# Predicting an edit: three projections opened during the modulation of a hybrid SSD and convolution layer

## The chip, the cores and the metric

One Trainium2 chip, one of its cores. The metric is the device time of one execution in microseconds (us); lower is better. Engines are named as the profile does: PE is TensorE, DVE VectorE, ACT ScalarE, POOL GpSimd, SP SyncE.

## What is computed

One trunk layer over 512 latent tokens and 256 context tokens of 1024 channels, fp32. The edit concerns its first steps:

```
mod   = silu(c) @ w_mod + b_mod          # the same for the context with c_ctx; split in shift, scale, gate
h     = rms_norm(x, norm_w) * (1 + scale) + shift
h_ctx = the same for the context tokens
proj  = h @ w_in                         # dt (step sizes), xs, B, C, z, glu, cg, gates; h_ctx @ w_in for dt, xs, B
dt    = softplus(dt_raw + dt_bias);  la = cumsum(dt * a) within chunks of 128
```

Behind them come a bidirectional state space mixer in eight groups of heads, a convolution module, gates, an output projection, the residual and a last norm. All that is the same in both kernels.

## The kernel before, in words

Everything is one function, `hybrid_block`. A scheduler puts the instructions of each engine into one fixed order when the program is built, and each engine then runs its own list in order.

*The start.* The modulation weights come in four blocks (`load_mod`, L198) of 1024 x 512: 256 channels of shift and of scale. SP loads block 0, the tokens `xt`, block 1, the context `ct`, block 2, and later block 3 and the first weights. For each block q, PE multiplies the two conditioning vectors (padded to 4 columns, `scf`) with the weights into `mp` (L249), DVE copies it to `ms` (L251), four transposes (`tp`, L254) bring it to the partitions, and DVE adds halves and bias (`md`) and makes the scale `s` (L263). Meanwhile ACT squares the tokens (L223), `rsqrt_small` makes the root, ACT scales the tokens (L227, L229). Then, for each of the two 128-channel blocks k of q, PE transposes the tokens (`hp`, L267), ACT (tokens, L272) or DVE (context, L270) applies scale and shift into `hf`, and `split` (L163, L164) makes a rounded fp32r half on ACT and its remainder on DVE: `hx[0]`, `hx[1]`, `hc[0]`, `hc[1]`.

*The projections.* `proj` (L322) takes a weight block of 128 output channels (`wblock`, L149: a rounded half `whi` on ACT, the remainder `wlo` on DVE) and sums over all eight k: three 512-column products for the tokens (L330, L331, L335) and, where the context is needed, three of 256 columns (L333, L334, L337). Two accumulators `px` and one `pc` are in rotation. The order of weight blocks is dt, then for each group xs, xs, B, C, z, z and so on.

*The step sizes.* From dt's sums ACT and DVE go through some ten small steps (L348 to L365), PE transposes and sums them (`tpd`, `pl`, `lt`, `pr`, `pt`, L370 to L394), `la` goes through DRAM, and ACT makes `wend` and `dec` (L398 to L402). Then the first group's `conv` copies xs0's and xs1's accumulators out (`pad`, L160).

Of the kernel before, what the change touches and what calls it, by code (L numbers as in the profile page):

```python
# [46 lines left out]
SPLIT_K = ()  # L47
# [32 lines left out]
def hybrid_block(ctx: ExitStack, tc: tile.TileContext, x, cx, pack, wmod, bgate, wall, fnw, out):  # L80
# [15 lines left out]
    def pv(name):  # L96
        o, w = OFF[name]
        return pk[:, o:o + w]
# [94 lines left out]
    with tc.tile_pool(name="st", bufs=1, reuse_waits="tile") as st, tc.tile_pool(name="stp", bufs=1, space=PSUM) as stp:  # L193
        xt = st.tile([P, NCH, D], F32, name="xt")
        ct = st.tile([P, NCC, D], F32, name="ct")
        wms = []

        def load_mod(q):  # L198
            wm = st.tile([P, KO, 512], F32, name="wm", tag="wm", bufs=3)
            for hf in range(2):  # L200
                nc.sync.dma_start(out=wm[:, 4 * hf:4 * hf + 4], in_=wmod[q, :, hf * 2048:(hf + 1) * 2048].rearrange("p (k c) -> p k c", k=4))
            wms.append(wm)

        load_mod(0)
        for t in range(0, NCH, 2):
            nc.sync.dma_start(out=xt[:, t:t + 2], in_=x[t * P:(t + 2) * P, :].rearrange("(t p) d -> p t d", p=P))
        load_mod(1)
        nc.sync.dma_start(out=ct, in_=cx.rearrange("(t p) d -> p t d", p=P))
        load_mod(2)
        sc = st.tile([P, KO, 2], F32, name="sc")  # L210
        table = S.activation(sc, pv("cT").rearrange("p (k two) -> p k two", two=2), AF.Silu)
        S.copy(scs[:, :, 0], sc)
        V.tensor_sub(scs[:, :, 1], sc, scs[:, :, 0].bitcast(F32))
        scf = st.tile([P, KO, 2, 2], F32, name="scf")
        V.memset(scf, 0.0)
        V.tensor_copy(scf[:, :, 0], sc)
        table = log_exp_table(table)
        ss = st.tile([P, NCH + NCC], F32, name="ss")
        junk = st.tile([P, D], F32, name="junk", tag="junk", bufs=2)
        for t in range(NCH + NCC):  # L220
            src = xt[:, t] if t < NCH else ct[:, t - NCH]
            junk = st.tile([P, D], F32, name="junk", tag="junk", bufs=2)
            S.activation(junk, src, AF.Square, accum_out=ss[:, t:t + 1])  # L223
        rx = rsqrt_small(st, "rx", ss[:, 0:NCH], 1.0 / D, table)
        rc = rsqrt_small(st, "rc", ss[:, NCH:], 1.0 / D, table)
        for t in range(NCH):
            S.mul(xt[:, t], xt[:, t], rx[:, t:t + 1])  # L227
        for t in range(NCC):
            S.mul(ct[:, t], ct[:, t], rc[:, t:t + 1])  # L229

        for q in range(4):
            if q == 1:
                load_mod(3)
                prefetch()
                prefetch()
            wm = wms[q]
            mp = stp.tile([4, 512], F32, name="mp", tag="mp", bufs=2)
            for k in range(0, KO, 2):
                if k in SPLIT_K:
                    wmh = st.tile([P, 2, 512], F32R, name="wmh", tag="wmh", bufs=2)  # L240
                    wml = st.tile([P, 2, 512], F32R, name="wml", tag="wml", bufs=2)
                    split(wmh, wml, wm[:, k:k + 2])
                for j in range(2):
                    if k in SPLIT_K:
                        st_ = scs[:, k + j].rearrange("p a b -> p (a b)")
                        T.matmul(mp, st_, wmh[:, j], start=(k + j == 0), stop=False)
                        T.matmul(mp, st_, wml[:, j], start=False, stop=(k + j == KO - 1))
                    else:
                        T.matmul(mp, scf[:, k + j].rearrange("p a b -> p (a b)"), wm[:, k + j], start=(k + j == 0), stop=(k + j == KO - 1))  # L249
            ms = st.tile([4, 512], F32, name="ms", tag="ms", bufs=2)  # L250
            V.tensor_copy(ms, mp)  # L251
            tp = stp.tile([P, 2, 2, 2, 2], F32, name="tp", tag="tp", bufs=1)
            for j in range(4):
                T.transpose(tp[:, j // 2, j % 2].rearrange("p a b -> p (a b)"), ms[:, j * P:(j + 1) * P], ident[0:4, 0:4])  # L254
            td = st.tile([P, 2, 2, 2, 2], F32, name="td", tag="td", bufs=2)
            V.tensor_copy(td, tp)
            md = st.tile([P, 2, 2, 2], F32, name="md", tag="md", bufs=2)
            V.tensor_add(md, td[:, :, :, 0], td[:, :, :, 1])
            V.tensor_add(md, md, pv("bmod").rearrange("p (s k) -> p s k", s=2)[:, :, 2 * q:2 * q + 2].unsqueeze(3).broadcast_to([P, 2, 2, 2]))
            for j in range(2):  # L260
                k = 2 * q + j
                s1 = st.tile([P, 2], F32, name="s1", tag="s1", bufs=4)
                V.tensor_scalar(s1, md[:, 1, j, :], 1.0, pv("normw")[:, k:k + 1], op0=ALU.add, op1=ALU.mult)  # L263
                for which, srct, n, dst in ((0, xt, NCH, hx), (1, ct, NCC, hc)):
                    hp = stp.tile([P, n * P], F32, name=f"hp{which}", tag=f"hp{which}", bufs=2)
                    for t in range(n):
                        T.transpose(hp[:, t * P:(t + 1) * P], srct[:, t, k * P:(k + 1) * P], ident)  # L267
                    hf = st.tile([P, n * P], F32, name=f"hf{which}", tag=f"hf{which}", bufs=2)
                    if which:
                        V.tensor_scalar(hf, hp, s1[:, which:which + 1], md[:, 0, j, which:which + 1], op0=ALU.mult, op1=ALU.add)  # L270
                    else:
                        S.activation(hf, hp, AF.Identity, scale=s1[:, which:which + 1], bias=md[:, 0, j, which:which + 1])  # L272
                    split(dst[0][:, k, :], dst[1][:, k, :], hf)

# [8 lines left out]
    taps = []  # L283
# [38 lines left out]
    def proj(pool, kind, idx, with_ctx=False, psx=None):  # L322
# [5 lines left out]
        for k in range(KO):  # L328
# [7 lines left out]
            if with_ctx:  # L336
                T.matmul(pc, lo[:, k, :], hc[0][:, k, :], start=False, stop=last)  # L337
        return px, pc

    if True:  # L340
        pp_stack = ctx
        pp = pp_stack.enter_context(tc.tile_pool(name="pp", bufs=1, space=PSUM, reuse_waits="tile"))
# [507 lines left out]
```

## Time and profile before

| what | us |
|---|---|
| runs, median of 3 (lowest, highest) | 947.39 (946.71, 948.42) |
| the profiled execution, span from first to last instruction | 945.1 |
| PE busy within the span | 923.5 |
| first modulation product | 6.52 |
| first projection product (dt) | 47.86 |
| first product of B | 73.78 |

The profile gives the profiled execution's time as its span; the runs' median is 2.3 us above it, which is what lies around the span. An engine's busy time is the time in which at least one of its instructions is in flight. Matmuls overlap each other, so a product's own length is longer than its step, the time from its start to the next one's.

### The profile page before, as it was taken

The page shows a single profiled execution, that of the slowest core. Times are in us where ns is not written, and L with a number is a line of the kernel's source. Part 1 is how long each engine was busy: PE and PEld are TensorE (multiplying, and loading weights), DVE is VectorE, ACT ScalarE, POOL GpSimd, SP SyncE. Part 2 cuts the span into 40 slices and gives each one's busy share as a digit, 9 for nine tenths or more (in the row PEclk, how much of TensorE's full clock was granted, in tenths as well). Part 3 has the DMA queues.
Part 4 walks back from the last instruction along what each step waited for, and adds up shares of the span by engine and source line. Part 5 has one row for each costly group of instructions (what it writes and reads, how often), then busy time and mean ns, then how long its engine had stood idle before and what let it go on. Part 6 is the DMA issues. An engine that isn't in the chain of part 4 may idle for free.

```text
span 945.1 us, 12712 instructions
## 1 busy us (share of the span) xinstructions
PE 923.5 (98%) x4695; PEld 735.2 (78%) x4695; DVE 735.6 (78%) x1232; ACT 529.5 (56%) x935; POOL 9.2 (1%) x115
## 2 busy tenths in 40 slices
PE   6999999999999999999999999999999999999996
PEld 1388788788788788787887887788888877778886
DVE  1667499997699994899994999789999964557933
ACT  5738946767667668468477667444523345424322
POOL 0000000000000000000000000000000000000000
PEclk9999999999999999999999999999999999999999
DMA  9524512512422324225124122366633345647622
GB/s 375 204 77 139 178 46 88 169 68 93 142 68 99 116 96 152 75 68 179 44 91 178 34 84 95 127 200 209 201 113 132 114 163 179 200 153 268 203 77 80
DMA packets 41376, 127.07 MB, mean 134 GB/s; under 512 B 4545, under 2 KB 4961, under 8 KB 40290
## 3 DMA queue, kind: packets, MB, share of 16 engines
q1 hardware_dynamic: 25040, 93.22, 28.5%
q10 hardware_dynamic: 16274, 33.04, 10.1%
q8 instruction: 37, 0.61, 0.3%
q14 instruction: 25, 0.20, 0.1%
HBM read 112.46 MB, written 13.78 MB: 134 GB/s over the span
## 4 chain that ended last, share of the span: by engine, by line
PE 84%; ACT 11%; DMA 3%; issue 2%; DVE 1%; SPq 0%; ACTq 0%
PE px L331 14%; PE px L335 14%; PE px L330 14%; PE px L764 5%; PE yo L568 3%; PE po L608 3%; PE po L607 3%; PE po L606 3%; PE mp L249 3%; ACT el L490 3%; PE pc L333 2%; PE pc L337 2%; PE pc L334 2%; PE yd L561 2%; ACT whi L154 2%; PE cp L529 2%
## 5 line engine op out<-in xcount | busy, mean ns | idle before, releaser
L330 PE MATMUL px<-hx,whi 128*128 128x512 f32 x712 | 284.9, 400 | 0.0
L331 PE MATMUL px<-hx,whi 128*128 128x512 f32 x712 | 282.4, 397 | 0.0
L335 PE MATMUL px<-hx,wlo 128*128 128x512 f32 x712 | 281.2, 395 | 0.0
L154 ACT CAST whi<-raw 128x1024 fp32r<-128x1024 f32 x121 | 126.1, 1047 | 169.1 <-PE px L331 61.7
L155 DVE TENSOR_TENSOR wlo<-raw,whi 128x1024 fp32r<-128x1024 f32 x121 | 147.1, 1221 | 72.4 <-ACT whi L154 69.7
L314 DVE SCALAR_TENSOR_TENSOR ac<-up,pk,ac 128x512 f32<-128x512 f32 x232 | 162.0, 745 | 0.0
L330 PEld LDWEIGHTS px<-hx,whi 128*128 128x128 f32 x712 | 133.9, 188 | 28.4 <-issue 0.5
L331 PEld LDWEIGHTS px<-hx,whi 128*128 128x128 f32 x712 | 133.9, 188 | 24.7 <-issue 3.1
L335 PEld LDWEIGHTS px<-hx,wlo 128*128 128x128 f32 x712 | 133.8, 188 | 22.8 <-issue 0.7
L550 ACT ACTIVATE tm<-slm,dtT 128x128 f32<-128x128 f32 x128 | 40.6, 391 | 53.9 <-DVE slm L542 45.3
L477 ACT ACTIVATE e<-la,laN 128x128 f32<-128x128 f32 x128 | 40.2, 393 | 36.5 <-PE yd L561 35.0
L333 PE MATMUL pc<-hc,whi 128*128 128x256 f32 x200 | 57.1, 286 | 0.1
L337 PE MATMUL pc<-hc,wlo 128*128 128x256 f32 x200 | 56.6, 283 | 0.0
L334 PE MATMUL pc<-hc,whi 128*128 128x256 f32 x200 | 56.5, 282 | 0.0
L606 PE MATMUL po<-yhi,whi 128*128 128x512 f32 x128 | 51.1, 399 | 0.0
L422 DVE SCALAR_TENSOR_TENSOR xsT<-pad,pk,xsT 128x771 f32<-128x771 f32 x48 | 48.8, 1016 | 2.4 <-ACT xsT L420 2.4
L608 PE MATMUL po<-yhi,wlo 128*128 128x512 f32 x128 | 50.6, 395 | 0.0
L607 PE MATMUL po<-ylo,whi 128*128 128x512 f32 x128 | 50.6, 395 | 0.0
L333 PEld LDWEIGHTS pc<-hc,whi 128*128 128x128 f32 x200 | 37.6, 188 | 7.2 <-issue 0.7
L334 PEld LDWEIGHTS pc<-hc,whi 128*128 128x128 f32 x200 | 37.6, 188 | 6.5
L490 ACT ACTIVATE el<-la 64x512 f32<-64x512 f32 x64 | 40.0, 625 | 0.5
L337 PEld LDWEIGHTS pc<-hc,wlo 128*128 128x128 f32 x200 | 37.6, 188 | 0.5 <-issue 0.5
(273 smaller groups left out, 1405.8 us busy)
## 6 DMA issues: line engine op xcount, KB each, us to landing
raw<-in_wall SPq DMA_DIRECT2D x121, 512.0 KB, 3.3
la<-la_d SPq DMA_DIRECT2D x32, 512.0 KB, 4.3
wm<-in_wmod SPq DMA_DIRECT2D x8, 1024.0 KB, 14.4
y_d<-y ACTq DMA_DIRECT2D x16, 256.0 KB, 2.0
yl<-y_d ACTq DMA_DIRECT2D x16, 256.0 KB, 3.4
raw<-in_wall ACTq DMA_DIRECT2D x8, 512.0 KB, 4.3
xt<-in_x SPq DMA_DIRECT2D x2, 1024.0 KB, 10.3
t_d<-t ACTq DMA_DIRECT2D x8, 256.0 KB, 2.4
```

What stands on the lines that cost most here:

```text
L154: S.copy(hi, raw)
L155: V.tensor_sub(lo, raw, hi.bitcast(F32))
L314: V.scalar_tensor_tensor(out=a, in0=up[:, :, t:t + GRID], scalar=cwh[:, d, t:t + 1], in1=a, op0=ALU.mult, op1=ALU.add)
L330: T.matmul(px, hi[:, k, :], hx[0][:, k, :], start=first, stop=False)
L331: T.matmul(px, hi[:, k, :], hx[1][:, k, :], start=False, stop=False)
L333: T.matmul(pc, hi[:, k, :], hc[0][:, k, :], start=first, stop=False)
L334: T.matmul(pc, hi[:, k, :], hc[1][:, k, :], start=False, stop=False)
L335: T.matmul(px, lo[:, k, :], hx[0][:, k, :], start=False, stop=last)
L337: T.matmul(pc, lo[:, k, :], hc[0][:, k, :], start=False, stop=last)
L606: T.matmul(ps, hi[:, k, :], rhi[:, i], start=(i == 0), stop=False)
L607: T.matmul(ps, hi[:, k, :], rlo[:, i], start=False, stop=False)
L608: T.matmul(ps, lo[:, k, :], rhi[:, i], start=False, stop=(i == 2 * KO - 1))
```

## The change

Five things, all at the start:

- The tokens are loaded first, then modulation blocks, now eight of 1024 x 256 (one 128-channel block k each, four buffers), with dt's and xs0's weights between the first of them.
- A modulation product is made in four column groups: `scf` is padded to 32 columns, and the eight row blocks i go to the PSUM partitions 32j to 32j + 31 with j = i mod 4. The four partial sums are added, and brought to the partitions, by a product with `sel`, a 128 x 2 selector.
- Squares and scalings of the tokens alternate between ACT and DVE.
- Three accumulator pairs are open during the loop over k: dt (in `yd` and half of `yo`), xs0 (`px`, `pc`), xs1 (`px`, the other half of `yo`). As soon as block k of `hx` and `hc` is there, the products of block k of all three are issued. `proj` returns these sums later (`opened`).
- All PSUM tiles of the start come from the one pool `pp`: `mp` and `hp` share the two buffers `m`.

```diff
-SPLIT_K = ()
+OPEN = (("dt", 0), ("xs", 0), ("xs", 1))
...
-    with tc.tile_pool(name="st", bufs=1, reuse_waits="tile") as st, tc.tile_pool(name="stp", bufs=1, space=PSUM) as stp:
...
-            wm = st.tile([P, KO, 512], F32, name="wm", tag="wm", bufs=3)
...
-        load_mod(0)
-        for t in range(0, NCH, 2):
-            nc.sync.dma_start(out=xt[:, t:t + 2], in_=x[t * P:(t + 2) * P, :].rearrange("(t p) d -> p t d", p=P))
-        load_mod(1)
...
-                        T.matmul(mp, scf[:, k + j].rearrange("p a b -> p (a b)"), wm[:, k + j], start=(k + j == 0), stop=(k + j == KO - 1))
...
+    def proj(pool, kind, idx, with_ctx=False):
+        if (kind, idx) in opened:
+            return opened.pop((kind, idx))
...
+            wm = st.tile([P, KO, 2 * P], F32, name="wm", tag="wm", bufs=4)
...
+        for t in range(NCH):
+            nc.sync.dma_start(out=xt[:, t], in_=x[t * P:(t + 1) * P, :])
+        load_mod(0)
+        prefetch()
+        load_mod(1)
+        prefetch()
+        nc.sync.dma_start(out=ct, in_=cx.rearrange("(t p) d -> p t d", p=P))
+        load_mod(2)
+        load_mod(3)
...
+        scf = st.tile([P, KO, 32], F32, name="scf")
+        V.memset(scf, 0.0)
+        V.tensor_copy(scf[:, :, 0:2], sc)
+        sel = st.tile([P, 2], F32, name="sel")
...
+        def square(t, src):
+            if t % 2:
+                junk = st.tile([P, D], F32, name="junkv", tag="junkv", bufs=1)
+                V.scalar_tensor_tensor(out=junk, in0=src, scalar=1.0, in1=src, op0=ALU.mult, op1=ALU.mult, accum_out=ss[:, t:t + 1])
...
+        for n, (kind, idx) in enumerate(OPEN):
+            if n == 0:
+                px = pp.tile([P, L], F32, name="px", tag="yd", bufs=1)
+                two = pp.tile([P, 2, L], F32, name="pc2", tag="yo", bufs=1)
+                pc = two[:, 0, 0:LC]
+            else:
+                px = acc_tile()
+                pc = two[:, 1, 0:LC] if n == 2 else pp.tile([P, L], F32, name="pc", tag="pc", bufs=1)[:, 0:LC]
...
+        for k in range(KO):
+            wm = wms[k]
+            mp = pp.tile([P, L], F32, name="mp", tag="m", bufs=2)
+            for i in range(KO):
+                j = i % 4
+                T.matmul(mp[32 * j:32 * j + 32, 0:2 * P], scf[:, i], wm[:, i], start=(i < 4), stop=(i >= 4))
+            if k + 4 < KO:
+                load_mod(k + 4)
+            ms = st.tile([P, 2 * P], F32, name="ms", tag="ms", bufs=2)
+            V.tensor_copy(ms, mp[:, 0:2 * P])
+            tp = mp[:, 2 * P:2 * P + 4].rearrange("p (s i) -> p s i", s=2)
+            for s_ in range(2):
+                T.matmul(tp[:, s_], ms[:, s_ * P:(s_ + 1) * P], sel, start=True, stop=True)
...
+            for which, srct, n, dst in ((0, xt, NCH, hx), (1, ct, NCC, hc)):
+                hp = pp.tile([P, L], F32, name=f"hp{which}", tag="m", bufs=2)[:, 0:n * P]
...
+                for n, (kind, idx) in enumerate(OPEN):
+                    if n == len(parts):
+                        parts.append(wblock(kind, idx))
+                    hi, lo = parts[n]
+                    into = grown[n][which]
+                    first, last = k == 0, k == KO - 1
+                    T.matmul(into, hi[:, k, :], dst[0][:, k, :], start=first, stop=False)
+                    T.matmul(into, hi[:, k, :], dst[1][:, k, :], start=False, stop=False)
+                    T.matmul(into, lo[:, k, :], dst[0][:, k, :], start=False, stop=last)
```

Where the instructions land is the scheduler's choice, so three places of the order are shown.

PE in the new kernel, block 4 of the loop, from the first token transpose on. `hp` are transposes, `mp<-sel,ms` the selector, `mp<-wm,scf` the product of block 5, `px` and `pc` the open projections (`pc_177` those of dt and xs1).

```order
L352 MATMUL hp_424<-ident,xt 128x128 x4
L344 MATMUL mp<-sel,ms 128x2 x2
L352 MATMUL hp_442<-ident,ct 128x128 x2
L337 MATMUL mp<-wm,scf 32x256
L365 MATMUL pc_177<-hc_100,whi 128x256
L365 MATMUL pc<-hc_100,whi 128x256
L337 MATMUL mp<-wm,scf 32x256 x4
L365 MATMUL px<-hx_95,whi 128x512 x2
L366 MATMUL px<-hx_96,whi 128x512
```

Sixteen further projection products follow, then three more of `mp<-wm,scf`, then block 5's transposes. In the kernel before, no projection stood in this part.

PE before, in the middle of xs0 and xs1, where the step sizes' transposes stand (`tpd`).

```order
L335 MATMUL px<-hx_95,wlo 128x512
L337 MATMUL pc<-hc_100,wlo 128x256
L330 MATMUL px<-hx_95,whi 128x512
L331 MATMUL px<-hx_96,whi 128x512
L370 MATMUL tpd<-ident,da 128x64 x6
L370 MATMUL tpd<-ident,dtv 128x64 x6
L335 MATMUL px<-hx_95,wlo 128x512
L330 MATMUL px<-hx_95,whi 128x512
```

PE in the new kernel, from the last product of the open projections on (`L251` is B's first product).

```order
L367 MATMUL pc_177<-hc_100,wlo 128x256
L397 MATMUL tpd<-ident,da 128x64 x6
L397 MATMUL tpd<-ident,dtv 128x64 x6
L405 MATMUL pl<-daT,tu 128x128
L406 MATMUL pl<-daT,tl 128x128
L413 MATMUL lt<-ident,laP 64x128 x4
L418 MATMUL pr<-daT,sl 128x192
L419 MATMUL pr<-daT,su 128x192
L421 MATMUL pt<-daT,ones 128x384
L251 MATMUL px<-hx_95,whi 128x512
```

What stood among the projections of xs0 and xs1 now stands between them and B, with nothing in between.

## Rows read from the trace of the kernel before

**Rows 1.** The page: the span, and busy time by engine.

```profile
span 945.1 us, 12712 instructions
...
PE 923.5 (98%) x4695; PEld 735.2 (78%) x4695; DVE 735.6 (78%) x1232; ACT 529.5 (56%) x935; POOL 9.2 (1%) x115
```

**Rows 2.** Busy us by engine (xinstructions), PEclk, DMA share, by stretch.

```profile
20.00:30.00 10.00, 10.00 (x37) 2.96 (x38) 2.44 (x8) 7.71 (x13) 0.00 (x0) 1.00 1.03 426
40.00:48.00 8.00, 8.00 (x32) 2.85 (x32) 6.81 (x16) 5.07 (x8) 0.00 (x0) 1.00 0.41 130
```

**Rows 3.** Timeline of PE: start us, length us, engine, line, operation, xcount.

```profile
6.52 8.56 PE L249 MATMUL mp<-wm,scf 128*4 128x512 f32 x16 [6.52 <-DMA wm<-in_wmod]
...
39.99 6.17 PE L249 MATMUL mp<-wm,scf 128*4 128x512 f32 x14
...
47.86 0.48 PE L330 MATMUL px<-hx,whi 128*128 128x512 f32 x1
...
49.24 0.39 PE L331 MATMUL px<-hx,whi 128*128 128x512 f32 x1
49.47 0.28 PE L333 MATMUL pc<-hc,whi 128*128 128x256 f32 x1
49.59 0.28 PE L334 MATMUL pc<-hc,whi 128*128 128x256 f32 x1
```

**Rows 4.** Timeline of ACT and DVE, token norms at the start.

```profile
11.47 1.06 ACT L223 ACTIVATE junk<-xt 128x1024 f32<-128x1024 f32 x1 [6.24 <-DMA xt<-in_x]
...
17.24 0.16 DVE L174 TENSOR_SCALAR rxm<-ss 128x4 f32<-128x4 f32 x1
...
18.70 4.26 ACT L227 ACTIVATE xt<-xt,rxr 128x1024 f32<-128x1024 f32 x4 [0.83 <-DVE rxr L184]
```

**Rows 5.** The page's costliest groups: the weight split.

```profile
L154 ACT CAST whi<-raw 128x1024 fp32r<-128x1024 f32 x121 | 126.1, 1047 | 169.1 <-PE px L331 61.7
L155 DVE TENSOR_TENSOR wlo<-raw,whi 128x1024 fp32r<-128x1024 f32 x121 | 147.1, 1221 | 72.4 <-ACT whi L154 69.7
```

**Rows 6.** Groups by line and form, 0 to 48 us: busy us, mean ns.

```profile
L272 ACT ACTIVATE hf<-hp,md,s 128x512 f32<-128x512 f32 x6 | 4.6, 775 | 4.6 <-DVE s L263 2.0 <-DVE rct L182 1.4 <-PE hp L267 1.3
...
L163 ACT CAST hx<-hf 128x512 fp32r<-128x512 f32 x6 | 3.7, 613 | 0.0
...
L164 DVE TENSOR_TENSOR hx<-hf,hx 128x512 fp32r<-128x512 f32 x6 | 4.1, 686 | 3.0 <-ACT hx L163 3.0
...
L270 DVE TENSOR_SCALAR hf<-hp,s,md 128x256 f32<-128x256 f32 x6 | 3.0, 538 | 0.0
L251 DVE COPY ms<-mp 4x512 f32<-4x512 f32 x4 | 2.7, 677 | 18.1 <-PE mp L249 18.0
```

**Rows 7.** Timeline, from a modulation transpose to the affine step that waits for it.

```profile
39.65 0.41 PE L254 MATMUL tp<-ident,ms 4*128 4x4 f32 x4
...
41.03 0.78 ACT L272 ACTIVATE hf<-hp,md,s 128x512 f32<-128x512 f32 x1 [2.01 <-DVE s L263]
```

**Rows 8.** Timeline: step sizes' first step, B's first product, xs1's last.

```profile
57.10 0.67 ACT L348 ACTIVATE dr<-px,pk 64x512 f32<-64x512 f32 x1
...
73.78 0.51 PE L330 MATMUL px<-hx,whi 128*128 128x512 f32 x1
...
77.07 0.28 PE L337 MATMUL pc<-hc,wlo 128*128 128x256 f32 x1
```

**Rows 9.** Timeline of PE: fp32 products on the full array, and on halves.

```profile
124.92 1.50 PE L568 MATMUL yo<-cT,sn 128*128 128x128 f32 x12
...
128.91 0.44 PE L561 MATMUL yd<-e,xtok 128*64 128x128 f32 x4
129.28 0.51 PE L331 MATMUL px<-hx,whi 128*128 128x512 f32 x1
```

**Rows 10.** Stretches after PE's last product at 937.6 us, columns as in rows 2.

```profile
938.00:940.00 2.00, 0.00 (x0) 0.00 (x0) 0.96 (x4) 0.81 (x4) 0.00 (x0) 1.00 0.00 0
942.00:945.00 3.00, 0.00 (x0) 0.00 (x0) 0.00 (x0) 0.00 (x0) 0.00 (x0) 0.50 0.47 175
```

More of the change, by code (lines that the diff above doesn't have):

```diff
@@ L190, in hybrid_block @@
     hc = [hcpool.tile([P, KO, LC], F32R, name=f"hc{i}") for i in range(2)]
-    with tc.tile_pool(name="st", bufs=1, reuse_waits="tile") as st, tc.tile_pool(name="stp", bufs=1, space=PSUM) as stp:
[L194 to L198, printed above, removed]
-            wm = st.tile([P, KO, 512], F32, name="wm", tag="wm", bufs=3)
-            for hf in range(2):
-                nc.sync.dma_start(out=wm[:, 4 * hf:4 * hf + 4], in_=wmod[q, :, hf * 2048:(hf + 1) * 2048].rearrange("p (k c) -> p k c", k=4))
-            wms.append(wm)
-        load_mod(0)
-        for t in range(0, NCH, 2):
-            nc.sync.dma_start(out=xt[:, t:t + 2], in_=x[t * P:(t + 2) * P, :].rearrange("(t p) d -> p t d", p=P))
-        load_mod(1)
[L208 to L248, printed above, removed]
-                        T.matmul(mp, scf[:, k + j].rearrange("p a b -> p (a b)"), wm[:, k + j], start=(k + j == 0), stop=(k + j == KO - 1))
[L250 to L273, printed above, removed]
@@ L276, in hybrid_block @@
+    pp = ctx.enter_context(tc.tile_pool(name="pp", bufs=1, space=PSUM, reuse_waits="tile"))
     pxt, pxn = ["px"], [0]
@@ L281, in acc_tile @@
         return pp.tile([P, L], F32, name="px", tag=tag, bufs=2 if tag == "px" else 1)
-    taps = []
+    taps, opened = [], {}
     def fill(n):
@@ L320, in hybrid_block @@
     GT, AC = [1], [1]
-    def proj(pool, kind, idx, with_ctx=False, psx=None):
+    def proj(pool, kind, idx, with_ctx=False):
+        if (kind, idx) in opened:
+            return opened.pop((kind, idx))
         hi, lo = wblock(kind, idx)
@@ L340, in hybrid_block @@
     if True:
-        pp_stack = ctx
-        pp = pp_stack.enter_context(tc.tile_pool(name="pp", bufs=1, space=PSUM, reuse_waits="tile"))
         with tc.tile_pool(name="dtp", bufs=1, reuse_waits="tile") as dp:
@@ L828, in layout @@
     wm = f["w_mod"][0]
-    blocks = [np.concatenate([wm[:, q * 256:(q + 1) * 256], wm[:, D + q * 256:D + (q + 1) * 256]], axis=1) for q in range(4)]
-    wmod = np.stack([b.reshape(KO, P, 512).transpose(1, 0, 2).reshape(P, -1) for b in blocks])
+    blocks = [np.concatenate([wm[:, k * P:(k + 1) * P], wm[:, D + k * P:D + (k + 1) * P]], axis=1) for k in range(KO)]
+    wmod = np.stack([b.reshape(KO, P, 2 * P).transpose(1, 0, 2).reshape(P, -1) for b in blocks])
     return {
```

48 lines of the change are left out of this document (added).

## The prediction, made before the changed kernel had run

> **What bounds the kernel now.** I read the page first, then the start by stretches, then single rows of PE, and last the two engines that feed PE. The page says TensorE is busy 98% of a 945.1 us span [rows 1]: a microsecond of PE work taken away, or of PE waiting added, is a microsecond of the result. The edit touches only the start, so the price is read there. From 20 to 30 us and from 40 to 48 us PE is busy in every microsecond [rows 2], and what fills it is the modulation product: a 512-column fp32 instruction every 0.43 us (13 steps and one length of 0.59 make 6.17), 16 of them for each of the four modulation blocks, 27.5 us in all [rows 3]. The loads are done by then (a DMA share of 1.03 in the first of these stretches, 0.41 in the second [rows 2]). The first projection starts at 47.86, and its products run at one per 0.23 us (512 columns) and 0.12 us (256) [rows 3], so one block of channels of one projection with context costs 3 x 0.23 + 3 x 0.12 = 1.04 us, and dt, xs0 and xs1 together 25 us. While xs0 and xs1 run, ACT and DVE work off the chain of the step sizes: from its first step at 57.10 to B's first product at 73.78 are 16.7 us [rows 8], and PE does not wait for it, since it has xs0 and xs1. At 73.78 only xs1's 24 context products are left over (2.8 us, up to 77.2 [rows 8]), so I count 76.6 as the time at which PE stands before B with everything else done. The run has no waits of PE worth naming behind that, so the new kernel's total moves by the new time of this point, less 76.6.
>
> **What the change adds and removes.** Call T the time at which the last of the three open projections is complete. In the new order of PE the small products of the step sizes (tpd to pt) and all of B stand behind T. Nothing is left to cover the chain: the chain's first step needs dt's sum, which is now complete only 0.7 us before T, and B's accumulators are the ones that xs0 and xs1 hold until ACT copies them out behind the chain. I take the 16.7 us as measured, so B starts at T + 16.0, and **the shift is T - 60.6**. Two more weight splits now stand on ACT and DVE within the chain (1.05 and 1.22 us each [rows 5]); against them stand waits for PE's queue that go, and I set both at nothing.
>
> T is the sum of three stretches.
>
> *Up to block 1.* Tokens come first. From 6.52 to 11.47 us 2 MB land [rows 3, 4], 0.41 MB a microsecond (sizes from the shapes). So the tokens are there at 9.1, the first modulation block at 11.5, dt's weights at 12.8, xs0's at 16.7, the context at 19.2. The squares end at 10.3 and their root costs 1.5 (17.24 to 18.70 [rows 4]); two scalings of 1.07 each on ACT (4.26 us for four [rows 4]) end at 14.0, with the other two beside them on DVE. ACT's order then has dt's split (1.05 to 15.0), DVE's its other half (1.22 to 16.3 [rows 5]) ahead of the shift and scale; affine step, cast and remainder (0.78, 0.61, 0.69 [rows 6]) give the first hx block at 18.9. xs0's split follows to 20.4, then DVE's square of the context (1.3, an estimate from the 1.22 of the same size [rows 5]), the root and a scaling: 24.3. PE's queue holds the context's transposes ahead of block 1's product, so PE stands from 20.7 to 24.3 with xs0's and dt's first products done. Product 1, the first context projections and the rest bring block 1's first transpose to **27.3**.
>
> *One block.* Count from its first transpose. The last product's sum lands at 0.1; DVE copies it in 0.4 (half the columns of the 0.68 row [rows 6]); from the selector at 0.7 to the affine step the old chain took 1.38 us (39.65 to 41.03 [rows 7]) with a copy and an add more, so I take 1.1: 1.8. The context's transposes need the buffer that the shift and scale have just read, 1.5 to 1.9; its affine step (0.54 [rows 6]) ends at 2.5, and only that frees the buffer of the next product: **2.6 us**, with 1.1 us of work for PE in them (ten 128-column steps of 0.11 [rows 9]) and 1.5 us of standing. Behind that: three projections, 3 x 1.04 = **3.1 us**, and the product in three batches. Its price is the unknown. Without any overlap of column groups it is 16 instructions of half the columns, 16 x 0.215 = 3.4 us; with four groups fully side by side 0.9. The nearest row is yd, whose products fill 64 columns each: four instructions from 128.91 to the next product at 129.28 take 0.37 us [rows 9], where four on the full array take 4 x 0.11 = 0.44. The four end within 0.44 us with lengths of 0.27 and more [rows 9], so they run as two pairs 0.16 apart. That is 0.107 for 128 columns, 0.05 for weights, and 0.09 for leaving. For 256 columns a pass is then 0.27, a batch of two 0.54 plus 0.09, three batches **1.9 us**. I take this, because yd shows two groups at once. A block is 2.6 + 3.1 + 1.9 = 7.6 us.
>
> The skill prices it too. The Trainium skill, TensorE: Matmul & The Clock Gate, section "Measured speedup vs the span model", gives 2.38 times for three column groups of 512 columns. By that the product would cost 3.4 / 2.38 = 1.4 us, an estimate from that page, and the total would be 4 us lower than mine; by yd's bare ratio (0.44 to 0.37) it would be 2.9 us and the total 8 us higher. No run here shows four groups.
>
> *To T.* Blocks 4 to 6 take 7.6 each, 22.8. xs1's weights wait for the buffer of dt's and land near 28, so block 1 has 1.4 us less to do (6.2) and blocks 2 and 3 take that up, in 2 partly within the standing time (6.8 and 8.2): 21.2. The last block has no product behind it but waits for its hx remainder: 6.3. T = 27.3 + 21.2 + 22.8 + 6.3 = **77.6**, and the shift 17.0.
>
> *The clock.* After PE's last product at 937.6 the granted clock is still 1.00 up to 940, and 0.50 (1.2 of 2.4 GHz) from 942 [rows 10]. PE stands longer than that behind T, so I expect the chain's products and B's first at 1.2 GHz. At the start sixteen steps took 8.56 us where 16 x 0.43 make 6.9 [rows 3]: 1.7 us lost before the engine ran at full rate. I add that once for B, and 1.3 for the dozen small products that lie on the chain, at 0.11 more each [rows 9]: **3.0**.
>
> *At nothing.* The eight modulation loads on SP, four of which now wait for a product, with the weight loads queued behind them: 1 MB takes 2.5 us and a block 7.6, so a load issued four blocks ahead is there; without that cover each block would cost 2.5 at most. The fewer small steps on DVE lie beside PE. Behind B both kernels do the same.
>
> Sum: 945.1 + 17.0 + 3.0 = 965.1. The runs' median, 947.39, lies 2.3 above the profiled span, so **967 us**, slower by 2.1%. A measurement of this kernel tells about 0.2% (2 us) from no change.
>
> **The rivals.**
> - *Faster: PE never stands in the blocks.* Place: the wait between the selector and the next product. If other projections filled it, and four groups ran side by side (0.9 us and 0.2 of leaving), a block would be 3.1 + 1.1 + 1.1 = 5.3 us of work; eight from 11.5 give T = 53.9, a shift of -6.7, some 941. It decides at T = 60.6. For it: blocks 2 and 3 do hold leftovers to fill with. Against it: the order on PE is fixed, the first block alone stands 3.6 us for the context, and two buffers serve products and transposes alike. 5%.
> - *Half filled.* Blocks of 6.4 and a start 2 us sooner: T = 77.6 - 8.4 - 2 = 67.2, 957; somewhat better still it is no change. 10%.
> - *Column groups don't overlap,* so the change doesn't do what it says: 1.5 to 2 us more in each of eight blocks, 14 more, 981. Against it yd's pairs. 10%.
> - *Clock at 1.2 GHz in the blocks.* PE would work only some 80% of each block. The 25 us of projections would double and the products with them, +31, 998. Against it: from 20 to 48 us the clock was 1.00 [rows 2]. 3%.
>
> **How the numbers follow.** My forecast, 957 to 975, has 72%, its width from the product's price (8 up, 4 down) and the length of the standing time (1 us per block is 7). For 8 in 10 the range goes from 956, the half-filled case, to 982, the serial product. It leaves out the faster case, the better half of the half-filled one and the slow clock. Faster by over 0.2%: 0.05; within 0.2%: 0.03; slower: 0.92.
>
> **What would show it.** In the new profile: B's first product near 94 us against 73.8; an empty PE of over 10 us just ahead of it, with the step sizes' rows on ACT and DVE inside, and a lower clock at its end; selector products of successive blocks some 7.6 us apart; a batch of four column groups whose starts lie within hundredths of a microsecond. I am wrong if B starts before 75 us, if the blocks follow each other in under 6 us, or if PE has work while the step sizes are computed.

## The result, and the profile of the changed kernel

The changed kernel takes 975.13 us (median of 4 runs, 973.28 to 975.59), the kernel before beside it 947.58 (946.71 to 948.42): 1.0280 times as long, 95% interval 1.0262 to 1.0299. The forecast was 967 with 956 to 982 around it, and slower with a chance of 0.92; the narrower 957 to 975, which had 72%, is missed by 0.1 us. The profiled execution took 974.98, its span is 973.3: 28.2 us more than before [rows 1], where 20.0 were forecast.

The page of the changed kernel, span and busy time by engine:

```profile
span 973.3 us, 12889 instructions
...
PE 924.8 (95%) x4775; PEld 745.2 (77%) x4775; DVE 743.5 (76%) x1242; ACT 524.2 (54%) x926; POOL 9.2 (1%) x115
```

PE is busy as long as before (924.8 us against 923.5 [rows 1]), although its busy time with the modulation product has gone from 31.0 us to 15.9: the selector has come in (5.0 us), and part of the work now runs at a lower clock. The other 26.9 of the 28.2 us are time in which PE stands. The stretches show both (columns as in rows 2):

```profile
50.00:60.00 10.00, 9.11 (x59) 6.42 (x58) 2.48 (x6) 1.68 (x3) 0.00 (x0) 1.00 0.01 2
60.00:70.00 10.00, 9.11 (x54) 5.79 (x52) 2.47 (x6) 1.68 (x3) 0.00 (x0) 0.83 0.00 0
66.00:68.00 2.00, 2.00 (x7) 1.54 (x6) 0.00 (x0) 0.00 (x0) 0.00 (x0) 0.50 0.00 0
80.00:85.00 5.00, 4.04 (x12) 3.11 (x13) 1.98 (x5) 3.04 (x6) 0.00 (x0) 0.67 0.02 3
90.00:95.00 5.00, 0.00 (x0) 0.00 (x0) 4.02 (x5) 1.79 (x2) 0.00 (x0) 0.50 0.49 186
95.00:100.00 5.00, 2.74 (x17) 2.34 (x18) 2.98 (x9) 0.00 (x0) 0.16 (x3) 0.50 0.01 2
100.00:105.00 5.00, 3.56 (x10) 2.31 (x10) 2.05 (x5) 1.08 (x8) 0.71 (x7) 0.50 0.14 26
110.00:120.00 10.00, 10.00 (x60) 8.70 (x59) 8.20 (x20) 8.44 (x19) 0.30 (x5) 1.00 0.27 96
```

From 86 to 96 us PE is empty and its granted clock falls from 1.00 to 0.50 (1.2 of 2.4 GHz); from 95 to 105 it is busy for 6.3 us at 0.50, and from 110 on it is full at full clock. Within the loop, before 86, it is busy some 90%, and the clock is 1.00 from 50 to 60 but 0.83 from 60 to 70, with 0.50 in the middle of that (66 to 68). The timeline of PE, first the loop, then the stand behind it:

```profile
13.11 1.94 PE L337 MATMUL mp<-wm,scf 128*32 128x256 f32 x16 [13.11 <-DMA wm<-in_wmod]
...
25.72 0.69 PE L352 MATMUL hp<-ident,ct 128*128 128x128 f32 x2 [2.84 <-ACT ct L306]
26.34 1.92 PE L337 MATMUL mp<-wm,scf 128*32 128x256 f32 x10
...
30.68 0.66 PE L352 MATMUL hp<-ident,xt 128*128 128x128 f32 x4
...
44.70 1.07 PE L337 MATMUL mp<-wm,scf 128*32 128x256 f32 x16
...
53.15 0.66 PE L352 MATMUL hp<-ident,xt 128*128 128x128 f32 x4
...
54.62 0.44 PE L352 MATMUL hp<-ident,ct 128*128 128x128 f32 x2 [0.26 <-DVE md L346]
...
55.70 0.62 PE L337 MATMUL mp<-wm,scf 128*32 128x256 f32 x2 [0.64 <-DVE hf L355]
...
60.90 0.66 PE L352 MATMUL hp<-ident,xt 128*128 128x128 f32 x4
...
70.22 0.66 PE L352 MATMUL hp<-ident,xt 128*128 128x128 f32 x4
...
85.87 0.28 PE L367 MATMUL pc<-hc,wlo 128*128 128x256 f32 x1
96.10 0.87 PE L397 MATMUL tpd<-ident,da 64*128 64x64 f32 x6 [9.95 <-DVE da L392]
...
105.50 0.79 PE L251 MATMUL px<-hx,whi 128*128 128x512 f32 x1 [1.94 <-ACT pad L160]
```

The first transposes of a block (`hp` from `xt`) stand at 53.15 and 60.90: a block takes 7.75 us, and in it PE waits for `md` and `hf` (0.26 and 0.64 us). The last product of the open projections starts at 85.87, so T is 86.0. Then PE waits 9.95 us for `da`, and after the small products 1.94 for the copy `pad`, until B starts at 105.50 (73.78 before [rows 8]). What ACT, DVE and POOL do in that stand:

```profile
84.44 0.68 ACT L375 ACTIVATE dr<-px,pk 64x512 f32<-64x512 f32 x1
...
85.65 2.36 DVE L155 TENSOR_TENSOR wlo<-raw,whi 128x1024 fp32r<-128x1024 f32 x2 [3.10 <-ACT dr L375]
85.71 1.05 ACT L154 CAST whi<-raw 128x1024 fp32r<-128x1024 f32 x1 [0.59 <-PE pc L366]
...
86.67 0.46 ACT L376 ACTIVATE dr<-pc,pk 64x256 f32<-64x256 f32 x1
87.93 0.94 DVE L380 SCALAR_TENSOR_TENSOR na<-dr 64x768 f32<-64x768 f32 x1
...
90.18 1.04 ACT L154 CAST whi<-raw 128x1024 fp32r<-128x1024 f32 x1 [0.42 <-DMA raw<-in_wall]
91.13 0.84 ACT L386 ACTIVATE lnu<-uu 64x768 f32<-64x768 f32 x1
...
95.34 0.61 DVE L392 TENSOR_SCALAR da<-dtv,av 64x768 f32<-64x768 f32 x1
...
103.63 0.10 POOL L436 MEMSET pad<- 128x2 f32 x1 [5.74 <-PE pt L421]
...
104.81 0.64 ACT L160 COPY pad<-px 128x512 f32<-128x512 f32 x1
```

The chain of the step sizes starts with `dr` at 84.44. Two `whi` and three `wlo` splits of the next weights lie between its steps. The edges of `pad`, which POOL clears, wait for `pt`, a product that reads the chain's `daT` and nothing of `pad`. I read this so that `pad` lies on memory that the chain still uses.

### The profile page after: what moved, and what is told of

The parts are those of the page before. It is cut to its first block, busy times and chain, and to the rows that moved or that the text cites. A ratio compares the mean times of both kernels' runs of the same rounds, so it can differ in the third digit from the quotient of the medians.

```text
span 973.3 us, 12889 instructions
## 1 busy us (share of the span) xinstructions
PE 924.8 (95%) x4775; PEld 745.2 (77%) x4775; DVE 743.5 (76%) x1242; ACT 524.2 (54%) x926; POOL 9.2 (1%) x115
## 3 DMA queue, kind: packets, MB, share of 16 engines
q10 hardware_dynamic: 16274, 33.04, 10.1%
## 4 chain that ended last, share of the span: by engine, by line
PE 75%; ACT 11%; issue 1%; DMA 1%; DVE 1%; SPq 0%; ACTq 0%; DVEq 0%
PE px L252 13%; PE px L251 13%; PE px L256 13%; PE px L791 5%; PE yo L595 3%; PE po L633 3%; PE po L635 3%; PE po L634 3%; ACT el L517 3%; PE pc L254 2%; ACT whi L154 2%; PE pc L258 2%; PE pc L255 2%; PE yd L588 2%; PE cp L556 2%; PE px L767 2%
## 5 line engine op out<-in xcount | busy, mean ns | idle before, releaser
L251 PE MATMUL px<-hx,whi 128*128 128x512 f32 x688 | 275.5, 400 | 1.9 <-ACT pad L160 1.9
L252 PE MATMUL px<-hx,whi 128*128 128x512 f32 x688 | 273.5, 398 | 0.0
L256 PE MATMUL px<-hx,wlo 128*128 128x512 f32 x688 | 271.8, 395 | 0.0
L251 PEld LDWEIGHTS px<-hx,whi 128*128 128x128 f32 x688 | 129.6, 188 | 30.3 <-ACT pad L160 3.1
L252 PEld LDWEIGHTS px<-hx,whi 128*128 128x128 f32 x688 | 129.7, 188 | 24.1 <-issue 3.1
L256 PEld LDWEIGHTS px<-hx,wlo 128*128 128x128 f32 x688 | 129.6, 188 | 22.2 <-issue 0.7
L254 PE MATMUL pc<-hc,whi 128*128 128x256 f32 x176 | 50.4, 286 | 0.0
L258 PE MATMUL pc<-hc,wlo 128*128 128x256 f32 x176 | 50.0, 284 | 0.0
L255 PE MATMUL pc<-hc,whi 128*128 128x256 f32 x176 | 50.0, 284 | 0.0
L255 PEld LDWEIGHTS pc<-hc,whi 128*128 128x128 f32 x176 | 33.4, 190 | 6.1
L254 PEld LDWEIGHTS pc<-hc,whi 128*128 128x128 f32 x176 | 33.4, 190 | 6.0 <-issue 0.7
L505 DVE SCALAR_TENSOR_TENSOR e<-la,laN,e 128x128 f32<-128x128 f32 x128 | 36.0, 345 | 1.1 <-ACT e L504 1.1
```

The costliest lines, as they stand in the source:

```text
L251: T.matmul(px, hi[:, k, :], hx[0][:, k, :], start=first, stop=False)
L252: T.matmul(px, hi[:, k, :], hx[1][:, k, :], start=False, stop=False)
L254: T.matmul(pc, hi[:, k, :], hc[0][:, k, :], start=first, stop=False)
L255: T.matmul(pc, hi[:, k, :], hc[1][:, k, :], start=False, stop=False)
L256: T.matmul(px, lo[:, k, :], hx[0][:, k, :], start=False, stop=last)
```

## Experiments

A rate over before is the ratio of medians to runs of the kernel before on the same chip, as a percentage with its 95% interval; 0.1% is about 1 us. The changed kernel stands at +2.80%.

**1. One projection kept behind the loop.** dt and xs0 stay open, xs1 is projected as a whole behind the loop, with PSUM buffers given out accordingly.

```diff
-OPEN = (("dt", 0), ("xs", 0), ("xs", 1))
+OPEN = (("dt", 0), ("xs", 0))
```

> Only dt and xs0 stay open; xs1 is projected as a whole behind the loop, so its 48 products (8.3 us of PE) stand between the last open product and the step sizes' transposes. My theory (the step sizes' chain has lost its cover): the open projections are complete 8 us sooner, the chain keeps its length, so B's first product comes 8 to 10 us sooner and the time is 965 to 967 us against 975. Rival (the loss lies in the loop alone, the same products are only moved): B at the same time, 975 us.

Measured: 966.21 us, +1.79% (1.46 to 2.13). B's first product comes at 96.96 in place of 105.50, and PE waits 1.06 us for `da` in place of 9.95. Some 1.0% comes back, 9.6 us, which is about the length of xs1's own products (8 x 1.04 = 8.3 us): as cover for the chain they are worth their length.

**2. PE kept at work in the stand.** 38 products of 512 columns that nobody reads, behind the last open one.

```diff
+FILL = 38
...
+            idle = pp.tile([P, L], F32, name="idle", tag="m", bufs=2)
+            for i in range(FILL):
+                T.matmul(idle, hx[0][:, i % KO, 0:P], hx[0][:, KO - 1, :], start=(i == 0), stop=(i == FILL - 1))
```

> The changed kernel with 38 extra products of 512 columns behind the open projections, into a buffer nobody reads, so PE works instead of standing while the step sizes are computed (8.7 us at full clock). Theory (the low clock behind the standing time costs 3 to 5 us in the chain's small products and in B's first): 970 to 972 us. Rival (the clock is the main cause of the loss): 960 us or less. Rival (the clock costs nothing there): 975 us.

Measured: 974.37 us, +2.56% (2.19 to 2.94); not to be told from the change. The stretches of this kernel, columns as above:

```profile
90.00:95.00 5.00, 3.44 (x24) 2.48 (x23) 3.88 (x9) 0.00 (x0) 0.16 (x3) 1.00 0.33 105
95.00:100.00 5.00, 3.06 (x10) 1.84 (x10) 2.41 (x8) 0.72 (x5) 0.71 (x7) 0.64 0.14 26
```

The added products end at 91.8, and the clock is 1.00 until 95 but 0.64 from 95 to 100: they held the clock over the first of the chain's products, not over the later ones, so this run alone doesn't rule out the rival. From `dr` to B it takes 19.9 us (80.96 to 100.86) in place of 21.1, so the clock held over these first products is worth some 1.2 us. B comes 4.6 us earlier in all, mostly because T does in this execution (83.0 in place of 86.0), though the loop is the same; the clock falls in other blocks here. At the end of the span 1.5 of the 4.6 us are left (971.8 against 973.3). A bound comes from the rows of the change: behind T PE is busy for under 10 us at 0.50 (2.74 and 3.56 up to 105, and the first products of B), so the full clock there would give back less than 5 of the 28 us, an estimate.

**3. The product without column groups.** All eight row blocks go to one group of 32 columns, and the copy and the selector behind them read that one group; everything else is as in the change.

```diff
-                T.matmul(mp[32 * j:32 * j + 32, 0:2 * P], scf[:, i], wm[:, i], start=(i < 4), stop=(i >= 4))
+                T.matmul(mp[0:32, 0:2 * P], scf[:, i], wm[:, i], start=(i == 0), stop=(i == KO - 1))
```

> The changed kernel with the modulation product on one column group: the eight row blocks add up in the same 32 columns. Theory (the groups run side by side and are a gain within the change): a block's 16 instructions take 3.4 us in place of 1.1 to 1.7, eight blocks 14 to 18 us more, 989 to 993 us. Rival (the groups hardly overlap, or pay for their gain by switching): 975 us plus or minus 5.

Measured: 993.25 us, +4.64% (4.27 to 5.01). The timeline of PE in this kernel, first transposes of two blocks and the large batch between them:

```profile
44.17 0.66 PE L352 MATMUL hp<-ident,xt 128*128 128x128 f32 x4
...
51.31 2.78 PE L337 MATMUL mp<-wm,scf 128*32 128x256 f32 x12
54.02 0.66 PE L352 MATMUL hp<-ident,xt 128*128 128x128 f32 x4
```

A block takes 9.85 us in place of 7.75, and 12 instructions take 2.78 us where 16 took 1.07 in the change. The column groups do run side by side, and within the change they are a gain of 1.8%.

**4. Column groups alone.** The kernel before, with its four blocks of 512 columns, the product in column groups, and the selector in place of transposes and adds.

```diff
-            mp = stp.tile([4, 512], F32, name="mp", tag="mp", bufs=2)
...
+            mp = stp.tile([P, 512], F32, name="mp", tag="mp", bufs=2)
+            for k in range(KO):
+                j = k % 4
+                T.matmul(mp[32 * j:32 * j + 32], scf[:, k], wm[:, k], start=(k < 4), stop=(k >= 4))
```

> The kernel before with the column groups alone: four blocks of 512 columns, four groups, and the selector in place of transposes and adds; load order, buffers and projections as before. Theory (the product set the pace of the start before, and the loss comes from the loop by single blocks and the uncovered chain): the start is then set by the loads (done at 33 us) and the last block's chain, dt's first product near 38 us in place of 47.9, 936 to 939 us. Rival (the groups don't help where nothing else is changed): 947 us.

Measured: 950.39 us, +0.19% (0.02 to 0.36). My theory failed. PE is busy with the product for 16.9 us in place of 31.0, and dt's first product still comes at 46.04 (47.86 before [rows 3]). The timeline of PE in this kernel shows what came in its place:

```profile
16.57 1.92 PE L242 MATMUL mp<-wm,scf 128*32 128x512 f32 x2 [2.99 <-DMA wm<-in_wmod]
...
31.13 0.66 PE L257 MATMUL hp<-ident,xt 128*128 128x128 f32 x4 [1.93 <-ACT hf L262]
...
33.51 0.69 PE L257 MATMUL hp<-ident,ct 128*128 128x128 f32 x2 [0.90 <-ACT ct L231]
34.13 1.92 PE L242 MATMUL mp<-wm,scf 128*32 128x512 f32 x2
...
41.89 1.06 PE L242 MATMUL mp<-wm,scf 128*32 128x512 f32 x8
...
46.04 0.48 PE L320 MATMUL px<-hx,whi 128*128 128x512 f32 x1
...
```

PE now waits for the weights (2.99), for ACT's affine step (1.93) and scalings (0.90), and the last modulation products still stand in its fixed order behind the transposes of earlier blocks (34.13 and 41.89). In the kernel before all this lay under the product. A batch of eight instructions takes 1.06 us at 41.89, but 1.94 at 20.89: up to about 26 us the products come at half rate, where in the kernel before they do so only up to about 10.

**5. The new loop without open projections.**

```diff
-OPEN = (("dt", 0), ("xs", 0), ("xs", 1))
+OPEN = ()
```

> The new loop with no projection taken into it: the tokens first, eight modulation blocks of 256 columns, the products in column groups, squares and scalings shared between ScalarE and VectorE; the step sizes and the convolution inputs are projected behind it as before, so that two whole projections lie under the chain of step sizes again. My theory, that the change loses by the cover of that chain and by the stands inside a block which the open projections lengthen: 953 to 961, half or more of the 28 given back, and TensorE's stand between 86 and 110 of the span cut to a few us. Rival, that the loop by itself (a block every 7.5 us, bound by its chain of waits whatever is projected in it) is what costs: 968 to 976. Rival, that the projections in the loop were a gain and only the cover is lost: like the run that projected the last channel set behind the loop, 965 to 967.

Measured: 950.82 us, +0.38% (0.22 to 0.54), better than the theory's range. The timeline of PE, from one block's product to the next:

```profile
34.14 1.07 PE L337 MATMUL mp<-wm,scf 128*32 128x256 f32 x16
35.14 0.66 PE L352 MATMUL hp<-ident,xt 128*128 128x128 f32 x4
35.56 0.48 PE L251 MATMUL px<-hx,whi 128*128 128x512 f32 x1
...
38.16 1.07 PE L337 MATMUL mp<-wm,scf 128*32 128x256 f32 x16
```

The scheduler has drawn dt's products and the token half of xs0's into the loop by itself, into the gaps of the chain. A block takes 4.02 us (34.14 to 38.16) and PE doesn't wait. So the loop is not slow by itself: what costs is how the change puts the projections into it, and the cover that it takes from the chain. This run undoes both at once. PE still stands for 4.2 us between 60 and 80.

**6. Tokens first, alone.** The kernel before with `load_mod(0)` behind the tokens' loads.

```diff
-        load_mod(0)
         for t in range(0, NCH, 2):
             nc.sync.dma_start(out=xt[:, t:t + 2], in_=x[t * P:(t + 2) * P, :].rearrange("(t p) d -> p t d", p=P))
+        load_mod(0)
```

> The kernel before with the tokens loaded ahead of the first modulation block and nothing else moved. TensorE's first product then starts later by what the tokens' transfer takes; TensorE has no other work in that stretch, and the norms, which start earlier, are not waited for until the first block's transposes. Theory (the order of the loads is a cost that the change must win back): 950 to 954. Rival (the norms' earlier end gives it back): 946 to 948.

Measured: 948.84 us, +0.10% (-0.01 to 0.22). The theory is wrong: whatever the order of the loads costs by itself, it is some 2 us at most.

**7 and 8. Can column groups alone be made to pay?** To run 4, first the weights of dt and xs0 are loaded earlier, then in addition squares and scalings are shared between ACT and DVE.

```diff
         nc.sync.dma_start(out=ct, in_=cx.rearrange("(t p) d -> p t d", p=P))
+        prefetch()
         load_mod(2)
+        prefetch()
...
-                prefetch()
-                prefetch()
...
-            S.activation(junk, src, AF.Square, accum_out=ss[:, t:t + 1])
+            square(t, src)
```

> The kernel before with column groups, and the first two sets of projection weights loaded ahead of the last two modulation blocks. Before it, column groups alone left TensorE waiting on ScalarE's norms and on the weights' second parts (1.05 us at 48 of the span). If the weights' arrival held its end: 943 to 947. If ScalarE's chain of norms and scalings sets the start of the first projection, as the trace of column groups alone reads: 948 to 952, no change. If the modulation's later arrival costs more than the weights' earlier one gives: over 952.

> The run before this, with the squares and scalings of the token norms also shared between ScalarE and VectorE, as in the change. If ScalarE's chain is what took up the gain of the column groups: 937 to 944, faster than both kernels. If TensorE's fixed order (the products of the later modulation blocks stand behind the transposes of the earlier ones) or the loads set the start: 946 to 952.

Measured: 948.54 us, +0.04% (-0.12 to 0.20), and 948.29 us, +0.03% (-0.14 to 0.19). Neither differs from the kernel before. In the second PE is busy 913.6 us, 10 less than before, over a span of 945.1, the same as before. Its first projection product starts at 46.37, 1.5 us earlier than before, and these are gone by the end. The norms on ACT weren't all that held the start: up to 48 us PE still waits 10.1 us for `wm` to arrive and 4.2 for `hf`, ACT's affine step. Which of the two would give more wasn't tried.

**9. The copies that empty the accumulators ahead of the chain's end.** `pad` gets a pool of its own, so that it no longer writes memory that the chain reads, and xs0's and xs1's copies are issued before the chain's last steps.

```diff
+        padp = pad_stack.enter_context(tc.tile_pool(name="padp", bufs=1, reuse_waits="tile"))
...
+            held = []
+            for t in range(2):
+                x0, x1 = proj(pp, "xs", t, True)
+                held.append((x0, x1, padded(x0, x1)))
             V.tensor_copy(wend, pr)
```

> The changed kernel, with the padded copies of the two channel sets, which empty the PSUM blocks that the next projection (B) needs, given memory of their own and written ahead of the chain's last step. In the trace of the change B's first product waits for such a copy (1.94 us, released by the copy), and the copies stand on ScalarE behind the exponentials that end the chain of step sizes; the first of them writes memory that the chain still reads. Theory (what the chain holds up is those copies, not B itself): B's first product comes within 3 us of the last open product, at 87 to 89 of the span in place of 105.5, and the chain runs under B, C and the gate; 953 to 959. Rival (B's projection, or what follows it, needs the chain's results, so the stand only moves to a later place): over 968. Between: the chain's steps, now shared with the projections' splits, end later and cost a second, shorter stand: 960 to 967.

Measured: 971.13 us, +2.34% (2.13 to 2.55), near the rival. The timelines of this kernel, PE and ACT:

```profile
85.94 0.40 PE L251 MATMUL px<-hx,whi 128*128 128x512 f32 x1
...
111.26 0.80 PE L251 MATMUL px<-hx,whi 128*128 128x512 f32 x1 [7.54 <-ACT pad L160]
...
102.23 0.53 ACT L444 ACTIVATE wend<-wend 128x384 f32<-128x384 f32 x1 [6.71 <-DVE wend L443]
...
104.52 1.95 ACT L458 ACTIVATE xsT<-pad,pk 128x771 f32<-128x771 f32 x2
...
110.62 0.59 ACT L160 COPY pad<-px 128x512 f32<-128x512 f32 x1
```

B starts at 85.94, right behind T, 19.6 us earlier than in the change; the theory holds for this place. But then PE waits 7.54 us, until 111.26, for the copy that empties B's accumulators. That copy stands on ACT behind the chain's exponentials (102.23), the start of xs0's and xs1's convolution (104.52) and nine steps that wait for `la`. I read the edit so that it had to stand there, since it needs one of the two `pad` buffers, which hold xs0 and xs1 until their convolution; that wasn't tested. B and C now cover the chain, and nothing covers what follows it. Of 19.6 us, 4.4 arrive at the end: the stand has for the most part moved. The run has both parts of the edit at once, the memory of its own and the earlier place, and doesn't part them.

**10. The projections one block later.** `take(k)`, the eighteen products of block k (three projections, three products each, tokens and context), is issued behind the next block's product, selector and transposes.

```diff
                 split(dst[0][:, k, :], dst[1][:, k, :], hf)
-                for n, (kind, idx) in enumerate(OPEN):
...
+            if k:
+                take(k - 1)
+        take(KO - 1)
```

> The changed kernel, with each block's three projections issued one block later: behind the next block's modulation product, selector and transposes, so that they lie under the next block's chain of waits, and the product needs not be split into batches. In the run of the loop alone, where projections came into the loop in that way, a block took 4.03 us with a third fewer projection steps and TensorE without a wait. By the same rows a block here is 1.0 product, 0.4 selector, 1.0 transposes and 3.1 projections, 5.5 to 5.7 us in place of 7.6; seven blocks and a longer end put the last open product at 73 to 76 in place of 86; everything behind unchanged. Theory (the order within a block is what makes it long): 961 to 966. Rival (the chain of waits through the two shared PSUM buffers sets the block's length whatever the order): 972 to 976.

Measured: 958.91 us, +1.05% (0.82 to 1.27), better than the theory's range. The timeline of PE over a block, and a stretch:

```profile
51.99 1.07 PE L349 MATMUL mp<-wm,scf 128*32 128x256 f32 x16
52.99 0.66 PE L364 MATMUL hp<-ident,xt 128*128 128x128 f32 x4
...
53.72 0.50 PE L356 MATMUL mp<-sel,ms 128*128 128x2 f32 x4
...
58.35 0.65 PE L364 MATMUL hp<-ident,xt 128*128 128x128 f32 x4
...
50.00:60.00 10.00, 10.00 (x85) 7.80 (x84) 4.39 (x12) 2.80 (x6) 0.00 (x0) 1.00 0.01 2
```

The product is made in one batch of 1.07 us, projections of the block before lie between the selector and the affine step, and the block takes 5.36 us (52.99 to 58.35) with PE at full clock. The last open product starts at 71.03, 14.8 us earlier than in the change. The stand behind it is as long as it was: `tpd` waits 10.55 us for `da`. This one change of order gives back 1.75% (2.80 less 1.05), some 16.6 us of the 27.6.

**11. Both together.** The edits of runs 9 and 10.

> Both of these edits. If they are independent (one shortens the way to the last open product by 10 to 13 us, the other takes away the stand behind it): the sum of both gains, 940 to 947 against 947.5 of the kernel before, no longer slower. If the chain's end then sets the first group (its results needed before TensorE has run out of projections): 950 to 957.

Measured: 956.48 us, +0.82% (0.62 to 1.01). The two gains of 0.46% and 1.75% leave 0.59% if they add; this is a little below the interval. Against run 10 the copies give 0.23%, within the intervals of the two, so that they pay there isn't shown; PE waits 7.67 us for such a copy in this run too (at 94.33). The sum that I had expected was out of reach, since run 9 alone gave less than its theory.

**12. The loop without open projections, with the copies of run 9.**

> The new loop without open projections (950.8), with the padded copies ahead of the chain's end as above. That run's TensorE stood 5 us of 60 to 80 of the span and had a granted clock of 0.69 in the second half of it; both go if the copies were what was waited for. Theory: 941 to 946, faster than both kernels. Rival (the step sizes themselves are needed): 949 to 952.

Measured: 947.77 us, -0.04% (-0.22 to 0.15): no difference from the kernel before, where a gain was expected. Against run 5 it is a gain of 0.4%, about the 4.2 us that PE stood there. PE no longer stands between 60 and 80 us, but ACT then waits 3.21 us for `la`, at 80.21, and PE for short stands behind it. No version that ran is faster than the kernel before.

## Why the forecast held, and which of its terms were off

*The mechanism was right.* B's first product is late, PE is empty for 9.95 us and more ahead of it, the step sizes' rows lie in that stretch, and the clock is 0.50 at its end. Run 1 confirms the cover: with xs1 put back behind the loop 1.0% comes back. Of the signs, the blocks came (7.75 us where 7.6 were named). B came at 105.5 and not near 94, and PE was empty for 9.95 us and not over 10, then in short waits up to B.

*The column groups were priced nearly right.* Three batches were set at 1.9 us a block. They take 1.7 us (0.54, 0.57 and 0.56 from the start of a batch of two, eight and six to the next instruction). The working had a slip: by its own pieces of `yd` (0.16, 0.107 and 0.09, which make 0.36 of its 0.37) a batch is 0.27 + 0.215 + 0.09 = 0.58, and three are 1.7, as measured; the 1.9 counts the 0.05 for weights once too often in each. The rival that they don't overlap is refuted by run 3. The Trainium skill, TensorE: Matmul & The Clock Gate, section "Measured speedup vs the span model", gives 2.38 times for three groups, from which I had an estimate of 1.4 us. The trace goes beyond it for four: 16 instructions take 1.07 us in one batch, against 16 steps of 0.215 us, the serial price of the forecast, which is 3.2 times.

*A block was sized right, and explained too firmly.* 7.6 us were forecast, and 7.75 is the block at full clock (53.15 to 60.90): 2.55 up to the next product, 1.67 for its batches and 3.53 for the projections, against 2.6, 1.9 and 3.1. But I took the 2.6 us ahead of the next product as a wait set by the two shared buffers, and gave the rival in which PE never stands 5%, on the ground that PE's order is fixed. Run 10 has the same buffers and a block of 5.36 us, within 0.1 of that rival's 5.3 (its T is 71.1 and not the rival's 53.9, since its blocks start late and the first ones take longer). The order is fixed when the program is built, and another could have been chosen. In run 10's block the transposes and the selector take 0.92 us of PE, with projections between them, where the change has 2.55; the one batch takes 1.00, where the three take 1.67; the projections take the same. So the step that failed as an explanation is the 2.6 us of "standing" within the block: not the buffers make it, but that the block's own projections, which need its end, come next in the order. Run 10 gives back 16.6 of the 27.6 us; the forecast had the total nearly right with that order as a given.

*The way to T was too short: 77.6 against 86.0.* Four pieces make up the 8.4 us. Block 1's first transpose came at 30.68 and not at 27.3 (+3.4): the context's scaling ended 1.4 later, since the loads landed later than worked out (the last tokens at 10.56 and not 9.1, the first modulation block at 13.11 and not 11.5), and the products behind it came at half rate (10 instructions in 1.92 us at 26.34), some 2.0. Blocks 1 to 3 took 22.5 and not 21.2 (+1.3), blocks 4 to 6 24.8 and not 22.8 (+2.0), the last 8.0 and not 6.3 (+1.7). In each of the last three pieces the granted clock had fallen for a while (0.83 in 30 to 40 and in 60 to 70, 0.67 in 80 to 85), and the block at the second fall took 9.32 us (60.90 to 70.22) in place of 7.75. By the steps at half rate the three falls cost 1.4, 1.6 and 1.5 us, estimates, so with the 2.0 ahead of block 1 some 6.5 of the 8.4 us are the clock. The forecast had the clock in the blocks only as a rival, at 1.2 GHz throughout, at 3% and 998 us, and at nothing in the sum. What came is a part of it, in single blocks. This is the term of the sum that was most wrong.

*The chain was too short as well.* From `dr` to B 16.7 us were taken over from the kernel before; it took 21.1 (84.44 to 105.50), 4.4 more. Two steps of the kernel before show where:

```profile
58.37 0.94 DVE L353 SCALAR_TENSOR_TENSOR na<-dr 64x768 f32<-64x768 f32 x1
...
64.65 0.61 DVE L365 TENSOR_SCALAR da<-dtv,av 64x768 f32<-64x768 f32 x1
```

From `dr` to `na` it takes 3.5 us and not 1.3, from `na` to `da` 7.4 and not 6.3, and from `da` to B 10.2 and not 9.1. So 3.4 of the 4.4 us arise before the first of the chain's products. I had set "two more weight splits" at nothing. Two on ACT and three on DVE lie within the chain, and the rows show them in the way: `na` waits behind two `wlo` until 87.93 (0.8), `lnu` behind a `whi` until 91.13 (0.8), and the next DVE step behind a `wlo` (0.4). The context half of `dr` comes only at 86.67, 2.2 us behind the token half, where it was 0.6 before: dt's context products come among the last of the block, and a `whi` stands ahead of it on ACT. How much of this is the `whi` isn't shown. Behind `da` the chain's products run at half clock, and a `wlo` that stood there before (65.72) is gone; the net is 1.0, where the forecast had 1.3 in its clock term.

*The sum.* T was 8.4 off and the way from T to B 3.5 (19.5 against 16.0), the 3.0 for the clock are contained in these measured pieces, and 0.7 came back behind B: 8.4 + 3.5 - 3.0 - 0.7 = 8.2, the difference between 965.1 and 973.3. The two large misses point the same way, so that the range held is owed to its width and not to errors that cancel.

*What stays open.* The runs don't part the clock's share from the order's in the gain of run 10, since PE without waits also kept its clock from 36 us on. The two later falls of the change cost some 3 us by the estimate above, of the 14.8 by which run 10's T is earlier, so most of that is the order. Whether a third `pad` buffer, or the channel sets' convolution ahead of the chain's end, would turn run 9 into its full gain wasn't tried.

## What to carry to other kernels

When an edit draws work forward, ask what that work was hiding: here two projections were the only thing PE had to do while a chain of some 17 us ran on two other engines, and the chain started again at their end. When new products are put into a loop that has a chain of waits, issue them one turn late, behind the next turn's start; the same instructions took 7.75 us a turn in one order and 5.36 in the other. And a cheaper operation can give nothing where its length was the cover of something else: the column groups made the product three times cheaper at the same clock and the kernel before no faster.

## What the runs showed that was not expected

*The clock falls in a loop in which PE stands a little in each turn.* In the change PE is busy 9.11 us in each of the stretches from 50 to 60 and from 60 to 70; the clock is 1.00 in the first and 0.83 in the second, down to 0.50 from 66 to 68. Which blocks are hit differs between kernels with the same loop: in run 9 the stretches from 50 to 60 and from 70 to 80 have 0.83, and their blocks last 9.3 us. In run 10, where PE hardly stands (34.95 of 35 us busy from 36 to 71), it is 1.00 over this stretch.

*Four column groups are some three times faster.* 16 instructions of 256 columns take 1.07 us, and 8 of 512 take 1.06 (41.89 in run 4), where the serial steps are 3.4.

*The start runs at half rate for longer.* The first batch takes 1.94 us for the same (13.11), and the batch at 26.34 and the products up to 30 come at half rate too, though the row prints a granted clock of 1.00 there. The trace's first record of the clock is at 30.5 us, so that 1.00 rests on none; in the kernel before it is at 9.6, in run 10 at 35.5, and in each the steps come at full rate from then on. So in the change PE, which stands much of the time up to 25 us, reaches the full clock some 20 us later than in the kernel before.
